# An fp32 encoder layer on two inputs: x passes ordered behind the short norm, head norms behind the next product, four early pairs, eight output tiles

## The chip, the cores and the metric

One core of one Trainium2 chip runs the whole program. The time is the device time of one execution in microseconds, median of several runs. "Profiled execution" is one more execution with the hardware profiler on; all durations below are from it. PE is TensorE, DVE VectorE, ACT ScalarE, POOL GpSimd, SP the engine that issues the DMAs.

## The reference, cut to what matters

Two inputs go through one transformer layer with the same weights: a long one (1024 tokens) and a short one (512), each with 16 meta tokens in front. All in fp32.

```python
def trunk(x, ...):
    h = concat([meta, x])                       # 16 + n tokens, 1024 wide
    n = rms_norm(h, g_mix);  proj = n @ w_in    # qa | ka | va | qb | kb | vb
    # A: 8 query heads, 2 key heads; q and k normed per head, rotated (axial)
    qa, ka = rope(rms_norm(qa)), rope(rms_norm(ka))
    oa = softmax(qa @ ka.T / 8) @ va
    # B: 4 heads, two softmax maps each, difference weighted by lambda; q and k rotated, no head norm
    ob = rms_norm((softmax(q1 @ k1.T / 8) - lam * softmax(q2 @ k2.T / 8)) @ vb) * (1 - lam_init)
    h = h + concat([oa, ob]) @ w_out
    n = rms_norm(h, g_ffn)
    gate = conv3(n @ w_ff_gate) + conv_b        # depthwise, along the tokens
    h = h + (gelu(gate) * (n @ w_ff_up)) @ w_ff_down   # 2816 wide
    return rms_norm(h, g_final)[:, 16:]
```

## The kernel before

Everything lies transposed: features on the 128 partitions, tokens along the free axis, 8 blocks of features (`KT`) for the width of 1024. An fp32 product is made of three matmuls in a faster format: each operand is split into a high part (a cast on ACT, `split`, L105) and a low part (the rest, a subtraction on DVE or POOL, L106), and `mm3` (L111 to L113) issues high x high, low x high, high x low. One product of a 128-wide column of a weight with a chunk of tokens is `dense`: 8 blocks, 24 matmuls into one PSUM tile.

`projection(s)` makes the 18 columns of w_in for input s (s = 1 is the short one, s = 0 the long one). It first reads x block by block: ACT writes `xhi` (L216) and the square of x (L220), DVE `xlo` (L217). For the short input the squares are summed by PE (L223), for the long one POOL adds them into `acc` (L225). `rsqrt_newton` (three ACT steps L95 to L97, two DVE steps L98 and L99) turns the sums into `rstd`, which DVE scales at L236. Only then can a product leave PSUM: DVE writes t = product * rstd (L277 for queries and keys of group A, L295 for values). For group A ACT squares t (L279), a matmul with `ones_hd` sums over the head (L281), `rsqrt_newton` runs again, and `rotary` (DVE, POOL) rotates; the results go to DRAM. The products of the short input take PSUM tiles of the tag s (3 tiles, sums in t, 2 tiles), those of the long one of the tag mm (2 tiles). A weight's column comes through one tile `w_f`, and `w_hi`, `w_lo` have two.

The program order is: projection of the short input; its attention merged with the long input's projection; the long input's attention merged with the short one's output product and gated network; the rest; and at the end `conv_glu_long`, the long input's gated network. A scheduler turns this into one fixed list per engine, by program order and its own model of durations; PSUM and SBUF tiles with their counts (`bufs`) limit how far apart things can move. `tc.issue_after(ins)` adds an edge: what is issued inside comes behind `ins` in its engine's list or waits for it. So the long input's passes may stand among the short norm's steps.

`conv_glu_long` works on pairs of 128 hidden features. For each pair it makes gate and up, and stores the product `act` and its sums (`a_t`, POOL) to DRAM. Then come seven products with blocks of w_down and of act over 11 pairs each (q = 0 to 6, a Strassen scheme; the last one in two halves of 256 tokens). For q = 0 the first two pairs' operands (left half of w_down, first half of act) are loaded ahead of the rest, into tiles `w_f` of the weight pool (L979, L980); those of the other pairs come as `a` and `a_f` (L995) behind the stores of the last pair. For q = 5 the second block of each pair from the third on is split into tiles that stay, and q = 6 uses these; the first two pairs are split again in q = 6, for each half. Last, `norm` writes y = h * gain * rs (L1066 and L1067 on ACT and POOL for every fourth, L1069 on DVE) into 4 tiles, each stored by its own DMA (L1070).

Of the kernel before, what the change touches and what calls it, by code (L numbers as in the profile page):

```python
# [12 lines left out]
F32 = mybir.dt.float32  # L13
# [76 lines left out]
def rsqrt_newton(g, tp, out, src, w, eps=None):  # L90
# [6 lines left out]
    nc.scalar.activation(out, y, AF.Square)  # L97
    nc.vector.scalar_tensor_tensor(out=out, in0=src, scalar=eps, in1=out, op0=ALU.add, op1=ALU.mult)  # L98
    nc.vector.scalar_tensor_tensor(out=out, in0=out, scalar=-3.0, in1=y, op0=ALU.add, op1=ALU.mult)  # L99

# [8 lines left out]
def mm3(g, ps, whi, wlo, xhi, xlo, start, stop):  # L109
    nc = g.nc  # L110
    nc.tensor.matmul(ps, lhsT=whi, rhs=xhi, start=start, stop=False)  # L111
    nc.tensor.matmul(ps, lhsT=whi, rhs=xlo, start=False, stop=False)  # L112
    nc.tensor.matmul(ps, lhsT=wlo, rhs=xhi, start=False, stop=stop)  # L113


def dense(g, ps, w, xhi, xlo, c0, cw, order=range(KT)):

    for i, k in enumerate(order):
        mm3(g, ps, *block(w, k), xhi[k][:, c0:c0 + cw], xlo[k][:, c0:c0 + cw], i == 0, i == KT - 1)
# [64 lines left out]
def projection(ctx, g, s, side, tag, tag2):  # L184
# [22 lines left out]
    with tc.tile_pool(name=f"ps{s}", bufs=2, side=side, reuse_waits="tile") as sp:  # L207
# [4 lines left out]
        for k in range(KT):  # L212
# [3 lines left out]
            nc.scalar.activation(xhi[k], x, AF.Copy, scale=gk)  # L216
            nc.vector.scalar_tensor_tensor(out=xlo[k], in0=x, scalar=gk,  # L217
                                           in1=xhi[k].bitcast(F32), op0=ALU.mult, op1=ALU.subtract)
            sq = acc if k == 0 and s == 0 else x
            nc.scalar.activation(sq, x, AF.Square)  # L220
# [8 lines left out]
        for i, (c0, cw) in enumerate(chunks):  # L229
# [5 lines left out]
            rsqrt_newton(g, sp, rstd[:, c0:c0 + cw], ps, cw)  # L235
        nc.vector.tensor_scalar(out=rstd, in0=rstd, scalar1=-0.5, scalar2=None, op0=ALU.mult)  # L236
# [24 lines left out]

    tab = load_tables(0)
# [4 lines left out]
    def qk_a(j):  # L267
        w = first if j == KA else load_weight(g, wp, g.w_in[j], ahead=1, lo_engine=nc.gpsimd if s == 0 else None)
        gn = g.gain[:, V_GK:V_GK + 1] if j == KA else g.gain[:, V_GQ:V_GQ + 1]
        for c0, cw in chunks:  # L270
            if j == KA and c0 == 0:
                ps = first_ps
            else:
                ps = g.psum.tile(P, cw, tag)
                dense(g, ps, w, xhi, xlo, c0, cw)
            t = tmp("t", cw, bufs=2 + s)
            nc.vector.tensor_tensor(out=t, in0=ps, in1=rstd[:, c0:c0 + cw], op=ALU.mult)  # L277
            sq = tmp("sq", cw, tag="w", bufs=2 + s)
            nc.scalar.activation(sq, t, AF.Square)  # L279
            ps = g.psum.tile(P, cw, tag2)  # L280
            nc.tensor.matmul(ps, lhsT=g.ones_hd, rhs=sq, start=True, stop=True)  # L281
            hn = tmp("hn", cw, bufs=1)
            rsqrt_newton(g, tp, hn, ps, cw)
            nc.vector.scalar_tensor_tensor(out=t, in0=t, scalar=gn, in1=hn, op0=ALU.mult, op1=ALU.mult)
            rotary(j, c0, cw, t, *tab)
            yield 25 * cw

    def values(j):
        w = load_weight(g, wp, g.w_in[j], ahead=1, lo_engine=nc.gpsimd if s == 0 else None)
        dst, tail = g.v[s][0 if j == VA else 1 + j - VB], g.vt[s][0 if j == VA else 1 + j - VB]  # L290
        for c0, cw in chunks:
            ps = g.psum.tile(P, cw, tag)
            dense(g, ps, w, xhi, xlo, c0, cw)
            t = tmp("t", cw, bufs=2 + s)
# [35 lines left out]
    for i in range(4):  # L330
        for j in (KB + i, QB + i):
            w = load_weight(g, wp, g.w_in[j], ahead=1, lo_engine=nc.gpsimd if s == 0 else None)
            for c0, cw in chunks:
                ps = g.psum.tile(P, cw, tag)
# [1016 lines left out]
```

## Time and profile before

| | |
|---|---|
| runs | 2161.72, 2146.39, 2156.50 us, median 2156.5 |
| profiled execution | 2160.32 us, span 2158.5 us |
| mean granted TensorE clock | 0.977 |
| busy share PE, DVE, ACT, POOL | 95%, 80%, 54%, 26% |
| DMA, mean over the span | 137 GB/s |

The profile shows one execution. "Busy" counts the time in which an engine works on at least one instruction; matmuls overlap, so the duration of one is longer than the distance to the next. A row of the timeline has the start, the duration, the engine, the line of the kernel, the operation, output <- inputs, shapes, how many rows it stands for, and in brackets how long the engine stood idle before it and who ended that. In the table of waits stand who waited <- for whom: us in total, times, the longest. In the table by stretches stand the stretch, its length, the busy time and the number of instructions of each engine, the granted TensorE clock (1.00 is full speed), DMA's share and rate.

### The profile page before, as it was taken

Reading aid. Unit: us, or ns where it says so; the run is one execution under the profiler, and the core shown is the slowest. Engines: PE = TensorE matmul, PEld = TensorE weight load, DVE = VectorE, ACT = ScalarE, POOL = GpSimd, SP = SyncE. Lnnn points to the kernel's source line nnn. Section 1 sums busy time; section 2 is a strip of 40 time slices with the busy share of each in tenths; the row PEclk is TensorE's granted clock in tenths of the full one; section 3 lists DMA queues with packets and bytes.
Section 4 is the critical chain, followed back from the end, with each engine's and each line's share of the span. In section 5 each row is a group of like instructions: output and inputs, shape, how many; then the busy total and the mean of one; then the engine's idle time right before and its main releaser. Section 6 shows DMA issues by size and latency. Waiting matters only on the chain.

```text
span 2158.5 us, 35229 instructions
## 1 busy us (share of the span) xinstructions
PE 2060.6 (95%) x12302; PEld 1840.5 (85%) x12302; DVE 1728.6 (80%) x3788; ACT 1161.2 (54%) x2255; POOL 552.3 (26%) x480
## 2 busy tenths in 40 slices
PE   7899998999999999999999999988999999989997
PEld 6898888898887999999989999887887777778877
DVE  6877888866979888889998885578778878869786
ACT  6534565543667565666666765345444344335454
POOL 3464222354112000000000000421444444420112
PEclk9999999899999999999999999998999999999999
DMA  6555334446631222223352234995222322257443
GB/s 233 169 173 186 112 115 141 147 168 220 207 118 54 95 74 75 73 77 119 103 186 85 83 112 139 273 289 192 98 98 83 108 103 83 104 185 243 118 127 123
DMA packets 171426, 296.31 MB, mean 137 GB/s; under 512 B 21456, under 2 KB 90608, under 8 KB 170736
## 3 DMA queue, kind: packets, MB, share of 16 engines
q1 hardware_dynamic: 171248, 294.05, 41.9%
q8 instruction: 97, 1.59, 0.3%
q14 instruction: 81, 0.66, 0.1%
HBM read 211.13 MB, written 82.85 MB: 136 GB/s over the span
## 4 chain that ended last, share of the span: by engine, by line
PE 73%; DVE 13%; DMA 6%; issue 3%; ACT 3%; POOL 1%; SPq 1%; POOLq 0%; DVEq 0%; ACTq 0%
PE ps_mm L111 17%; PE ps_mm L113 16%; PE ps_mm L112 16%; PE ps_t L411 5%; PE ps_s L386 3%; PE ps_s L387 3%; DVE w_lo L106 2%; PE ps_o L426 2%; PE ps_o L425 1%; DVE p L388 1%; PE ps_s L111 1%; PE ps_s L113 1%; PE ps_s L112 1%; DVE acc L921 1%; DVE pt_lo L106 1%
## 5 line engine op out<-in xcount | busy, mean ns | idle before, releaser
L111 PE MATMUL ps_mm<-xhi,w_hi 128*128 128x258 f32 (+3 forms) x1264 | 390.4, 309 | 11.8 <-ACT xhi L216 6.7
L112 PE MATMUL ps_mm<-xlo,w_hi 128*128 128x258 f32 (+3 forms) x1264 | 382.1, 302 | 3.0 <-DVE xlo L217 2.2
L113 PE MATMUL ps_mm<-xhi,w_lo 128*128 128x258 f32 (+3 forms) x1264 | 380.3, 301 | 0.3 <-DVE w_lo L106 0.3
L388 DVE TENSOR_SCALAR_CACHE_REDUCE p<-ps_s 114x344 f32<-114x344 f32 (+4 forms) x562 | 257.1, 489 | 42.1 <-PE ps_s L387 23.3
L111 PEld LDWEIGHTS ps_mm<-xhi,w_hi 128*128 128x128 f32 x1264 | 242.6, 192 | 18.5 <-ACT xhi L216 7.2
L105 ACT CAST pt_hi<-ps_t 128x512 fp32r<-128x512 f32 (+6 forms) x360 | 170.3, 484 | 162.7 <-PE ps_t L411 136.2
L393 ACT ACTIVATE p<-p,nm 114x1040 f32<-114x1040 f32 (+5 forms) x212 | 215.0, 1014 | 78.5 <-DVE nm L391 77.5
L106 DVE TENSOR_TENSOR w_lo<-w_f,w_hi 128x1024 fp32r<-128x1024 f32 (+1 forms) x176 | 187.1, 1069 | 77.8 <-ACT w_hi L105 77.4
L112 PEld LDWEIGHTS ps_mm<-xlo,w_hi 128*128 128x128 f32 x1264 | 242.5, 192 | 7.0 <-DVE xlo L217 2.6
L113 PEld LDWEIGHTS ps_mm<-xhi,w_lo 128*128 128x128 f32 x1264 | 241.9, 191 | 1.4 <-DVE w_lo L106 0.5
L105 ACT CAST w_hi<-w_f 128x1024 fp32r<-128x1024 f32 (+1 forms) x193 | 164.0, 863 | 94.4 <-PE ps_mm L112 54.1
L106 DVE TENSOR_TENSOR pt_lo<-ps_t,pt_hi 128x512 fp32r<-128x512 f32 (+4 forms) x312 | 172.0, 562 | 29.6 <-ACT pt_hi L105 28.7
L386 PE MATMUL ps_s<-k,q 128*114 128x348 f32 (+4 forms) x552 | 182.8, 336 | 12.1 <-DVE p L388 11.5
L106 POOL TENSOR_TENSOR a_lo<-gate,a_hi 128x256 fp32r<-128x256 f32 x44 | 43.5, 990 | 551.6 <-ACT a_hi L105 532.0
L411 PE MATMUL ps_t<-ident,p 128*128 128x128 f32 (+7 forms) x1188 | 182.5, 269 | 0.7 <-DVE pt_lo L106 0.2
L387 PE MATMUL ps_s<-k,q 128*114 128x348 f32 (+4 forms) x552 | 172.4, 317 | 0.1
L411 PEld LDWEIGHTS ps_t<-ident,p 128*128 128x128 f32 (+7 forms) x1188 | 140.3, 136 | 28.0 <-issue 6.6
L111 PE MATMUL ps_s<-xhi,w_hi 128*128 128x256 f32 (+4 forms) x480 | 148.5, 312 | 15.6 <-ACT xhi L216 7.3
L113 PE MATMUL ps_s<-xhi,w_lo 128*128 128x256 f32 (+4 forms) x480 | 146.8, 307 | 3.5 <-DMA w_lo<-wo 3.1
L112 PE MATMUL ps_s<-xlo,w_hi 128*128 128x256 f32 (+4 forms) x480 | 147.9, 309 | 0.3
L111 PE MATMUL ps_mm<-t_hi,w_hi 128*128 128x512 f32 (+2 forms) x368 | 143.5, 390 | 1.3 <-ACT t_hi L105 1.3
L112 PE MATMUL ps_mm<-t_lo,w_hi 128*128 128x512 f32 (+2 forms) x368 | 143.7, 390 | 0.5 <-DVE t_lo L106 0.5
(265 smaller groups left out, 5299.4 us busy)
## 6 DMA issues: line engine op xcount, KB each, us to landing
w_f<-w_gate SPq DMA_DIRECT2D x46, 512.0 KB, 3.3
w_f<-w_up SPq DMA_DIRECT2D x44, 512.0 KB, 3.4
w_f<-w_in SPq DMA_DIRECT2D x36, 512.0 KB, 3.9
a_f<-act SPq DMA_DIRECT2D x64, 256.0 KB, 2.9
w_f<-w_down SPq DMA_DIRECT2D x22, 512.0 KB, 3.3
act<-a_t SPq DMA_DIRECT2D x44, 256.0 KB, 2.1
a<-w_down SPq DMA_DIRECT2D x42, 256.0 KB, 5.4
w_hi<-wo SPq DMA_DIRECT2D x36, 256.0 KB, 5.2
```

Of the source, the lines that this page charges most:

```text
L105: nc.scalar.copy(hi, src)
L106: (lo_engine or nc.vector).tensor_tensor(out=lo, in0=src, in1=hi.bitcast(F32), op=ALU.subtract)
L111: nc.tensor.matmul(ps, lhsT=whi, rhs=xhi, start=start, stop=False)
L112: nc.tensor.matmul(ps, lhsT=whi, rhs=xlo, start=False, stop=False)
L113: nc.tensor.matmul(ps, lhsT=wlo, rhs=xhi, start=False, stop=stop)
L386: nc.tensor.matmul(ps, lhsT=q[0], rhs=k[:, c0:c0 + cw], start=True, stop=False)
L387: nc.tensor.matmul(ps, lhsT=q[1], rhs=k[:, c0:c0 + cw], start=False, stop=True)
L388: nc.vector.tensor_scalar(out=p[:, c0:c0 + cw], in0=ps, scalar1=HD ** -0.5, scalar2=-3.0e38, op0=ALU.mult, op1=ALU.max, accum_out=mx[:, i: ...
L393: nc.scalar.activation(p, p, AF.Exp, bias=nm, accum_out=l)
L411: nc.tensor.transpose(tps[:, c:c + M], p[:, k0:k0 + kw], g.ident[:M, :M])
L425: nc.tensor.matmul(o, lhsT=v[:, i, :], rhs=hi, start=i == 0, stop=False)
L426: nc.tensor.matmul(o, lhsT=v[:, i, :], rhs=lo, start=False, stop=False)
```

## The change

1. `mm3`, `dense` and `rsqrt_newton` return their last instruction. The short input's projection leaves the last ACT step of its norm and the scaling by DVE in `g.norm_of_short`, and the long input's xhi, xlo and squares are issued after these.
2. A new `product` issues a pending head norm behind the last matmul of the next product; so the norm of a chunk (L281 to rotary) is written one product later. t has 3 tiles for both inputs, the square has 2 of its own.
3. Four pairs' operands for q = 0 are loaded early instead of two, the third and fourth into a new pool. In q = 5 every pair's second block is split into tiles that stay (the first four into the tiles of the early operands), so that q = 6 splits no weight.
4. The final norm has 8 y tiles instead of 4.

```diff
 def rsqrt_newton(g, tp, out, src, w, eps=None):
...
-    nc.scalar.activation(out, y, AF.Square)
+    last = nc.scalar.activation(out, y, AF.Square).ins
...
+    return last
...
+            with ExitStack() as order:
+                for ins in g.norm_of_short:
+                    order.enter_context(tc.issue_after(ins))
+                nc.scalar.activation(xhi[k], x, AF.Copy, scale=gk)
+                nc.vector.scalar_tensor_tensor(out=xlo[k], in0=x, scalar=gk,
+                                               in1=xhi[k].bitcast(F32), op0=ALU.mult, op1=ALU.subtract)
+                sq = acc if k == 0 and s == 0 else x
+                nc.scalar.activation(sq, x, AF.Square)
...
+            last = rsqrt_newton(g, sp, rstd[:, c0:c0 + cw], ps, cw)
+        scaled = nc.vector.tensor_scalar(out=rstd, in0=rstd, scalar1=-0.5, scalar2=None, op0=ALU.mult)
+        g.norm_of_short = [last, scaled.ins]
...
+    pending = []
+
+    def product(w, c0, cw):
+        ps = g.psum.tile(P, cw, tag)
+        last = dense(g, ps, w, xhi, xlo, c0, cw)
+        if pending:
+            with tc.issue_after(last):
+                pending.pop()()
+        return ps
...
-                ps = g.psum.tile(P, cw, tag)
-                dense(g, ps, w, xhi, xlo, c0, cw)
-            t = tmp("t", cw, bufs=2 + s)
+                ps = product(w, c0, cw)
+            t = tmp("t", cw, bufs=3)
...
-            sq = tmp("sq", cw, tag="w", bufs=2 + s)
+            sq = tmp("sq", cw, bufs=2)
...
+            def norm(c0=c0, cw=cw, t=t, sq=sq):
+                ps = g.psum.tile(P, cw, tag2)
+                nc.tensor.matmul(ps, lhsT=g.ones_hd, rhs=sq, start=True, stop=True)
+                hn = tmp("hn", cw, bufs=1)
+                rsqrt_newton(g, tp, hn, ps, cw)
+                nc.vector.scalar_tensor_tensor(out=t, in0=t, scalar=gn, in1=hn, op0=ALU.mult, op1=ALU.mult)
+                rotary(j, c0, cw, t, *tab)
+
+            pending.append(norm)
...
+    for f in range(NPRE):
+        if f % 2 == 0:
+            first_w += halves(f, F32)
+            first_x += halves(f + 1, F32)
+        nc.sync.dma_start(out=first_w[f], in_=g.w_down[2 * f][:, :H])
+        nc.sync.dma_start(out=first_x[f], in_=g.act[f, 0])
...
-            y = op.tile([P, H], F32, name="y", tag="y", bufs=4)[:, :cw]
+            y = op.tile([P, H], F32, name="y", tag="y", bufs=8)[:, :cw]
...
-            w = last[f] if q == 6 and f > 1 else split_half(g, wp, w)
+            w = last[f] if q == 6 else split_half(g, wp, w)
...
+NPRE = 4
```

How it moves the lists. ACT at the start of the program, behind the short input's squares; 256 and 272 are the short norm's two chunks, 1040 the long input's passes, 1024 weight casts. Before:

```order
L216 ACTIVATE xhi_1914<-x,vec 128x1040
L220 ACTIVATE acc<-x 128x1040
L95 ACTIVATE rs_y<-ps_t,eps 128x256
L216 ACTIVATE xhi_1915<-x,vec 128x1040
L96 ACTIVATE rs_y<-rs_y 128x256
L97 ACTIVATE rstd<-rs_y 128x256
L220 ACTIVATE x<-x 128x1040
L95 ACTIVATE rs_y<-ps_t,eps 128x272
L105 CAST w_hi<-w_f 128x1024
L96 ACTIVATE rs_y<-rs_y 128x272
L105 CAST w_hi<-w_f 128x1024
L97 ACTIVATE rstd<-rs_y 128x272
```

And after:

```order
L95 ACTIVATE rs_y<-ps_t,eps 128x256
L96 ACTIVATE rs_y<-rs_y 128x256
L97 ACTIVATE rstd<-rs_y 128x256
L95 ACTIVATE rs_y<-ps_t,eps 128x272
L96 ACTIVATE rs_y<-rs_y 128x272
L97 ACTIVATE rstd<-rs_y 128x272
L223 ACTIVATE xhi_1914<-x,vec 128x1040
L227 ACTIVATE acc<-x 128x1040
L223 ACTIVATE xhi_1915<-x,vec 128x1040
L106 CAST w_hi<-w_f 128x1024 x2
```

The six steps of the norm now stand together, ahead of every long pass. DVE at the same place, first before:

```order
L217 SCALAR_TENSOR_TENSOR xlo_1922<-x,vec,xhi_1914 128x1040
L217 SCALAR_TENSOR_TENSOR xlo_1923<-x,vec,xhi_1915 128x1040
L98 SCALAR_TENSOR_TENSOR rstd<-ps_t,eps,rstd 128x256
L99 SCALAR_TENSOR_TENSOR rstd<-rstd,rs_y 128x256
L106 TENSOR_TENSOR w_lo<-w_f,w_hi 128x1024
L98 SCALAR_TENSOR_TENSOR rstd<-ps_t,eps,rstd 128x272
L99 SCALAR_TENSOR_TENSOR rstd<-rstd,rs_y 128x272
L217 SCALAR_TENSOR_TENSOR xlo_1924<-x,vec,xhi_1916 128x1040
L236 TENSOR_SCALAR rstd<-rstd 128x528
L277 TENSOR_TENSOR t<-ps_s,rstd 128x256
```

and after:

```order
L98 SCALAR_TENSOR_TENSOR rstd<-ps_t,eps,rstd 128x256
L99 SCALAR_TENSOR_TENSOR rstd<-rstd,rs_y 128x256
L98 SCALAR_TENSOR_TENSOR rstd<-ps_t,eps,rstd 128x272
L99 SCALAR_TENSOR_TENSOR rstd<-rstd,rs_y 128x272
L243 TENSOR_SCALAR rstd<-rstd 128x528
L224 SCALAR_TENSOR_TENSOR xlo_1922<-x,vec,xhi_1914 128x1040
L295 TENSOR_TENSOR t<-ps_s,rstd 128x256
L295 TENSOR_TENSOR t<-ps_s,rstd 128x272
```

One xlo stands between the scaling and the first t, where two xlo and a weight's rest stood ahead of the second chunk's steps. On PE, the nine matmuls of the long product (ps_mm) that stood ahead of the short input's next product are four.

PE at the long input's last key chunk (272 tokens); `ones_hd` is the head norm's matmul. Before:

```order
L111 MATMUL ps_mm<-xhi_1921,w_hi 128x272
L112 MATMUL ps_mm<-xlo_1929,w_hi 128x272
L113 MATMUL ps_mm<-xhi_1921,w_lo 128x272
L281 MATMUL ps_mm<-sq,ones_hd 128x272
L111 MATMUL ps_mm<-xhi_1914,w_hi 128x384
```

and after:

```order
L113 MATMUL ps_mm<-xhi_1921,w_hi 128x272
L114 MATMUL ps_mm<-xlo_1929,w_hi 128x272
L115 MATMUL ps_mm<-xhi_1921,w_lo 128x272
L407 MATMUL ps_s<-k,q 128x264 x3
L301 MATMUL ps_mm<-sq,ones_hd 128x272
```

The norm's matmul stood right behind its product; now score matmuls of the short input's attention stand between (three, in one row), and the first scores come some 75 rows earlier in PE's list, ahead of that much of the long input's projection.

SP at the seam from the last gate/up pair to the down products; the a_t and act rows are stores, a_0 to a_4 the other halves of w_down. Before:

```order
L962 DMA act_108<-act 128x512
L962 DMA act_108<-a_t 128x512
L995 DMA a_2_23039<-w_down 128x512
L962 DMA act_108<-a_t 128x512 x2
L995 DMA a_f<-act_108 128x512
L995 DMA a_3_23063<-w_down 128x512
```

and after:

```order
L982 DMA act_108<-a_t 128x512 x2
L1025 DMA a_4_23090<-w_down 128x512
L1025 DMA a_4_23092<-w_down 128x512
L982 DMA act_108<-a_t 128x512
L1025 DMA a_f<-act_108 128x512
L1025 DMA a_5_23116<-w_down 128x512
```

The first a_f behind the stores belonged to the third pair; now it belongs to the fifth, at the same place behind the last store.

51 lines of the change are left out of this document (22 added, 29 removed).

## The prediction

> **What bounds the kernel now.** I read the page first (shares of the engines), then the busy time by stretches, then what TensorE waits for in the first stretch, and last the instructions of the places that the diff touches.
>
> ```profile
> PE 2060.6 (95%) x12302; PEld 1840.5 (85%) x12302; DVE 1728.6 (80%) x3788; ACT 1161.2 (54%) x2255; POOL 552.3 (26%) x480
> ```
>
> TensorE (PE) is busy in 95% of the span, so a change that adds no matmul can win only what PE stands idle, 2158.5 - 2060.6 = 98 us, and what it runs at a lowered clock. I cut the head of the program at 183.25 us, where the first score matmul of an attention stands:
>
> ```profile
> core 0: us, PE busy (x) PEld busy (x) DVE busy (x) ACT busy (x) POOL busy (x), PEclk, DMA share, GB/s
> 7.31:183.25 175.94, 157.41 (x1103) 149.62 (x1104) 128.59 (x202) 89.13 (x165) 93.08 (x82) 0.96 0.58 190
> 183.25:510.00 326.75, 309.22 (x1950) 288.60 (x1951) 258.34 (x780) 175.89 (x426) 117.72 (x109) 0.95 0.43 140
> 510.00:900.00 390.00, 378.78 (x2522) 338.90 (x2521) 325.32 (x896) 236.77 (x412) 55.04 (x70) 0.99 0.36 115
> ```
>
> In the head PE idles 175.94 - 157.41 = 18.5 us, almost a fifth of all its idle time in a twelfth of the span. Who ends these waits:
>
> ```profile
> PE ps_mm L111 <- ACT xhi L216: 6.7, 2, 4.3
> PE ps_mm L281 <- ACT sq L279: 3.8, 1, 3.8
> PE ps_t L281 <- ACT sq L279: 2.5, 2, 1.8
> PE ps_mm L112 <- DVE xlo L217: 2.2, 1, 2.2
> PE ps_s L111 <- DVE t L295: 1.9, 1, 1.9
> ```
>
> (columns: us in total, times, longest). Two things that the diff moves stand here: the long input's passes xhi and xlo, and the head norm's matmul L281, which waits for the square of the product that has only just ended. Idle time is not all; the clock falls behind some of these waits:
>
> ```profile
> 30.20:40.40 10.20, 6.68 (x26) 5.98 (x27) 6.93 (x9) 4.89 (x6) 8.27 (x4) 0.50 0.51 156
> 129.20:132.60 3.40, 3.40 (x12) 3.28 (x11) 3.25 (x9) 1.77 (x4) 3.40 (x3) 0.50 0.21 66
> ```
>
> PE worked 6.68 and 3.40 us there at a clock of 0.50, which costs half of that, 3.3 and 1.7 us. So the head can give at most 18.5 + 5.0 = 23.5 us.
>
> **Part 1: the short norm ahead of the long passes.** Before, ACT runs long passes of more than 1 us each between the six steps of the short norm, and DVE does the same:
>
> ```profile
> 23.12 0.46 ACT L95 ACTIVATE rs_y<-ps_t,eps 128x256 f32<-128x256 f32 x1
> 23.48 1.15 ACT L216 ACTIVATE xhi<-x,vec 128x1040 fp32r<-128x1040 f32 x1
> 26.39 0.42 DVE L99 SCALAR_TENSOR_TENSOR rstd<-rstd,rs_y 128x256 f32<-128x256 f32 x1
> 26.97 0.47 ACT L95 ACTIVATE rs_y<-ps_t,eps 128x272 f32<-128x272 f32 x1
> 30.00 0.43 ACT L97 ACTIVATE rstd<-rs_y 128x272 f32<-128x272 f32 x1
> 30.17 2.67 POOL L106 TENSOR_TENSOR w_lo<-w_f,w_hi 128x1024 fp32r<-128x1024 f32 x1 [0.63 <-ACT w_hi L105]
> 30.55 0.49 DVE L98 SCALAR_TENSOR_TENSOR rstd<-ps_t,eps,rstd 128x272 f32<-128x272 f32 x1
> 31.07 2.06 DVE L99 SCALAR_TENSOR_TENSOR rstd<-rstd,rs_y 128x272 f32<-128x272 f32 x1
> 33.06 1.29 DVE L217 SCALAR_TENSOR_TENSOR xlo<-x,vec,xhi 128x1040 fp32r<-128x1040 f32 x1
> 34.27 0.42 DVE L236 TENSOR_SCALAR rstd<-rstd 128x528 f32<-128x528 f32 x1
> 34.73 0.77 DVE L277 TENSOR_TENSOR t<-ps_s,rstd 128x256 f32<-128x256 f32 x2
> 35.21 0.29 PEld L111 LDWEIGHTS ps_s<-xhi,w_hi 128*128 128x128 f32 x1 [0.30 <-DVE t L277]
> ```
>
> The last row is the start of the short value product, which takes a PSUM buffer that t has read. From the first step at 23.12, six steps of 0.43 to 0.47 end at about 25.8. DVE then has L98 of the second chunk (0.49), L99 (0.42 where POOL is quiet), the scaling (0.42), one xlo that the new order leaves there (1.29) and the first t (about 0.4): 25.8 + 3.0 = 28.8, and PE starts at about 28.9 where it started at 35.21. Of the long product only four matmuls stand ahead of it instead of nine. The five have to be done later: at about 0.17 us each, half of the 0.33 us of overlapping rows, that is 0.9 us. 35.21 - 28.9 - 0.9 = 5.4 us. Of the stretch at 0.50 the part behind 35.21 (5.2 us, so 2.6 us lost) may go too, if the shorter wait of 28.9 - 27.3 = 1.6 us no longer lowers the clock (PE's idle time began 4.27 us before 31.53). Rows of this trace stand on both sides:
>
> ```profile
> 58.94 0.44 PE L111 MATMUL ps_mm<-xhi,w_hi 128*128 128x384 f32 x1 [2.39 <-ACT xhi L216]
> 330.49 0.76 PE L435 MATMUL ps_o<-pt_hi,v_tail 64*128 64x512 f32 x1 [2.22 <-DVE pt_hi L106]
> 58.00:66.00 8.00, 7.06 (x54) 6.89 (x54) 7.22 (x9) 5.87 (x11) 4.61 (x4) 1.00 0.78 274
> 330.50:337.30 6.80, 6.80 (x22) 6.34 (x23) 4.14 (x16) 3.50 (x9) 0.88 (x2) 0.50 0.41 139
> ```
>
> After 2.39 us of waiting the clock stayed at 1.00, after 2.22 us it was 0.50 for 6.8 us. So I take half, 1.3 us, and the part gives **6.7 us** (bounds: 5.4 and 8.0). [...]
>
> The added waits: every long xhi and square now stands behind ACT's L97, every xlo behind DVE's scaling. Behind them on ACT are weight splits, which the order moves back by about one; nobody waits for the long sums (POOL's adds) before 69 us. I cost that at nothing; if PE does run out there, it is what the first rival prices.
>
> **Part 2: head norms behind the next product.** No instruction is added; L281 waits 3.8 + 2.5 = 6.3 us in the head for ACT's square. With a whole product (24 matmuls; the 12 of the stretch at 129.20 took 3.40 us at half clock, so 24 take some 3 us at the full one) ahead of it that square is done, since t and the square are short (0.77 us for two t above); the 2.5 us go. The 3.8 us stand at the long input's last chunk, and the stretch at 129.20 (1.7 us) follows them, 5.5 together; there the new order puts three score matmuls ahead of the norm's, not a product, so I count 4.5. **7.0 us**; below it 3, if the later norms only shift the long wait to the scores, above it 8. The other idle times of the head (2.39 for xhi, 1.9 for t) I leave as they are, since t has three buffers in the short input as before.
>
> **Part 3: four pairs early.** At the seam from the last gate/up pair to the down products:
>
> ```profile
> 1923.95 1.93 SPq L962 DMA_DIRECT2D act<-a_t  x2
> 1925.92 0.46 SPq L995 DMA_DIRECT2D a_f<-act  x1
> 1930.69 0.62 ACT L105 CAST w_hi<-a_f 128x512 fp32r<-128x512 f32 x1 [12.93 <-DMA a_f<-act]
> 1931.88 2.08 PE L111 MATMUL ps_mm<-w_hi 128*128 128x512 f32 x4 [6.29 <-ACT w_hi L105]
> 1932.85 0.62 ACT L105 CAST w_hi<-a_f 128x512 fp32r<-128x512 f32 x1 [1.02 <-DMA a_f<-act]
> 1928.00:1934.80 6.80, 2.92 (x7) 2.36 (x8) 2.59 (x4) 2.28 (x4) 0.00 (x0) 0.50 0.96 312
> ```
>
> PE has two pairs preloaded, ends them at 1931.88 - 6.29 = 1925.59, and waits for the third, whose load SP issues behind the stores of a_t. Two more pairs are 24 matmuls of 0.227 us (the spacing of the last pair's rows), 5.4 us, and PE ends at 1931.0. The first pair that is still loaded late keeps its place in SP's queue behind the same stores, so PE starts it at 1931.9 and waits 0.9 us. Then pairs come every 1932.85 - 1930.69 = 2.2 us, and PE needs 2.7. Gain 5.4 us; the half clock there cost 2.92 / 2 = 1.5 us, of which I count 0.6: **6.0 us** (5 to 6.9). The early loads add no bytes, they move 1 MB (four tiles of 256 KB) ahead of the last gate/up pairs, which hide it; if PE waited for all of it there, it would be 3.4 us at the 312 GB/s of the last row.
>
> **Part 4: eight output tiles, no second split.** The tail:
>
> ```profile
> 2147.34 0.47 ACT L95 ACTIVATE rs_y<-ps_mm,eps 128x256 f32<-128x256 f32 x1 [1.02 <-PE ps_mm L1140]
> 2149.78 1.74 DVE L1069 SCALAR_TENSOR_TENSOR y<-c,gain,rs 128x256 f32<-128x256 f32 x3
> 2154.41 0.51 ACT L1066 ACTIVATE y<-u,gain 128x256 f32<-128x256 f32 x1 [5.24 <-DMA yT<-y]
> 2154.99 0.72 POOL L1067 TENSOR_TENSOR y<-y,rs 128x256 f32<-128x256 f32 x1 [4.15 <-ACT y L1066]
> L1070 SPq DMA_DIRECT2D yT<-y x16: 332/332/1501, 2139.8 to 2155.7; - x16
> ```
>
> The last product ends before 2147 whatever the tiles do. With a tile each, DVE's six y (0.48 each) run from 2149.78 to 2152.7, and SP's eight issues of 0.33 to 0.45 end at 2153.3, where the last started at 2155.7: **2.7 us** (2 to 3.2). The dropped splits of the last product lie beside PE's matmuls on ACT and DVE: nothing.
>
> **Sum.** 6.7 + 7.0 + 6.0 + 2.7 = 22.4 us. From the profiled execution, 2160.3 us, that is 2137.9, a ratio of 0.9896; on the median of the runs, 2156.5 (3.8 lower), 2134. For 183 to 900 us, where the order is reshuffled too, no term: PE's idle time there is 17.5 + 11.2 us and the clock costs about 15 more, and nothing shows which way these go. I bound it at 10 us to either side, about a quarter.
>
> **Rivals.**
> (1) *The head's waits are replaced.* DVE is at 128.59 of 175.94 us, and POOL lengthens it: L99 took 0.42 us at 26.39, but 2.06 beside POOL's 2.67 us of w_lo, while L98, which reads PSUM, kept 0.49 beside the same instruction. Packing the head tighter puts more DVE steps beside POOL. If six that PE then waits for are longer by 1.64, 9.8 us come back: total 12.6, time 2144. Against it: DVE stays under 80% even in a head of 162 us. [...]
> (2) *The attentions gain too*, because norms queue behind products there as well: 10 us more, 2124.
> (3) *Slower: the softmax step p comes late.*
>
> ```profile
> PE ps_s L386 <- DVE p L388: 11.5, 8, 3.9
> ```
>
> (from 183 to 900 us) Norms and rotaries of the long input, now issued later, stand ahead of p on DVE. One such wait is 1.4 us, and with 6.8 us at 0.50 behind it 4.8. Ten more than the eight of now eat 22.4 and cost another 25: 2182. From five more on the gain is gone. Against it: DVE gets about 10 us of work more in 183 to 510 (0.73 of the 13.7 us), 82% instead of 79.
> (4) *It doesn't do what it says*: the new edges bind only the order of issue, and if what PE waits for in the head turns out to be the loads of the long input behind those passes, parts 1 and 2 give nothing and 3 and 4 give 8.7: 2148. Against it: the waits above name ACT and DVE, and DMA's share is 0.51 in 30.20 to 40.40.
>
> **How the numbers follow.** Forecast 0.54 (its own range 2126 to 2143), (1) 0.20, (2) 0.12, (3) 0.06, (4) 0.08. A measurement of this kernel tells about 1% from no change: faster means under 2135, slower over 2178. The forecast lies across the first of these, somewhat more than half below, so faster 0.54 x 0.55 + 0.12 + 0.05 of (1) = 0.47; same 0.46; slower 0.07. The range takes in (1), (2) and (4) with some room: 2118 to 2151.
>
> **What would show it.** Right: TensorE's idle time between 27 and 36 us falls from about 6.8 us to under 3; no wait of the head norm's matmul over 0.5; the 6.29 at the seam becomes about 1; no output step waits for a yT load; the first score matmul, with the long work done before it counted in, about 14 us earlier. Wrong: new waits on t, p or w_lo in 40 to 510 us, more stretches at 0.50 there, or a seam that waits for the split of pairs three and four.

## The result, and the profile after

| | before | changed |
|---|---|---|
| median of 11 runs | 2150.27 us (2146.39 to 2164.51) | 2142.05 us (2132.45 to 2146.66) |
| ratio | | **0.9941** (0.9918 to 0.9965) |
| profiled execution | 2160.32 us | 2142.05 us |

The change makes the kernel faster, by about 12.7 us (0.0059 of 2150), where 22.4 was forecast. The ratio is that of the means, 2140.7 and 2153.3 us; the medians alone differ by 8.2. The profiled execution from which the prediction counted lies 10 us over its kernel's median; so the 18.3 us between the two profiles overstate the change.

The page of the changed kernel, engines:

```profile
PE 2046.2 (96%) x12302; PEld 1830.6 (86%) x12302; DVE 1738.0 (81%) x3786; ACT 1158.9 (54%) x2253; POOL 556.1 (26%) x480
```

TensorE still sets the time. Its idle time went from 97.9 to 2140.2 - 2046.2 = 94.0 us only; its busy time fell by 14.4 us for the same 12302 matmuls. Part of that is granted clock: 99.5 us of its record lay at 0.50 before, 83.3 after. In the kernel before, rows of 272 columns follow each other at 0.227 us in the stretch at 0.50 from 35.6 us on and at 0.126 where the clock is 1.00; at that ratio 16.2 us less at half clock are worth 7.2 us, an estimate. Where the other 7 us of busy time went the two traces do not name.

By stretches, the changed kernel (the columns are those of the prediction's table):

```profile
27.00:36.00 9.00, 9.00 (x68) 8.79 (x69) 8.57 (x8) 7.36 (x12) 9.00 (x4) 1.00 0.49 155
40.00:50.00 10.00, 6.92 (x36) 6.87 (x37) 9.88 (x14) 5.82 (x9) 6.10 (x5) 0.66 0.60 211
183.00:480.00 297.00, 288.66 (x1875) 270.79 (x1874) 248.90 (x734) 167.52 (x404) 114.55 (x101) 0.98 0.45 144
480.00:550.00 70.00, 49.96 (x291) 44.62 (x289) 43.43 (x137) 31.18 (x66) 11.05 (x17) 0.80 0.63 211
```

and the kernel before in the last two:

```profile
183.00:480.00 297.00, 279.22 (x1745) 258.66 (x1746) 241.38 (x748) 165.62 (x402) 100.06 (x93) 0.95 0.45 143
480.00:550.00 70.00, 64.66 (x386) 60.25 (x384) 48.99 (x139) 30.38 (x62) 26.44 (x28) 0.93 0.68 234
```

Between 27 and 36 us TensorE no longer idles at all, the aim of part 1. But it idles 3.1 us of the ten from 40 on, and between 480 and 550, where the program passes from the short input's attention to the long one's, it stands idle for 20 us and runs at 0.80. The attention, for which the prediction had no term, went the other way: 130 more matmuls in the same 297 us.

Since the order on TensorE changed, I compare executions by work: each matmul weighs its width plus 8 columns (an estimate; at a clock of 1.00 rows of 256 columns follow each other at 0.118 us and rows of 512 at 0.227, 0.45 and 0.44 ns for each column so counted), and the **lead** of a kernel at a time is how much later the profiled execution of before had done the same amount (us). It is worked out from the records of each trace. The kernels with parts left out or mended, which the table lists too, are described under the experiments.

| profiled execution | 35 | 50 | 183 | 480 | 550 | 1900 | 1935 |
|---|---|---|---|---|---|---|---|
| changed | 8.9 | 2.8 | 1.2 | 22.6 | 7.0 | 11.7 | 15.8 |
| changed, again | 8.8 | 2.5 | 2.1 | 26.0 | 11.6 | 17.6 | 21.5 |
| changed without part 2 | 7.4 | 2.5 | -1.8 | 14.6 | 15.6 | 24.1 | 29.7 |
| the same, again | 8.7 | 3.9 | -3.4 | 13.8 | 13.9 | 18.1 | 24.0 |
| changed without part 1 | 0.2 | 1.4 | -5.9 | 0.2 | 1.8 | 5.2 | 11.3 |
| parts 3 and 4 alone | 0.2 | 0.4 | 0.3 | 7.2 | 7.3 | 15.7 | 21.7 |
| the same, again | 0.2 | 0.6 | -1.7 | -1.4 | -1.3 | 1.9 | 5.9 |
| sums of POOL left out | 9.0 | 12.1 | 1.7 | 8.5 | 7.0 | 21.3 | 24.9 |
| changed, seam mended | 8.7 | 3.7 | 4.6 | 27.8 | 16.3 | 18.5 | 24.2 |
| the same, again | 7.4 | 2.2 | -0.8 | 23.3 | 12.4 | 17.1 | 22.0 |

The two rows of parts 3 and 4 warn the reader: up to 1850 us those two executions and that of before have the same list on TensorE, and yet they lie up to 16 us apart. Differences below some 10 us count only where a pair of rows agrees.

The head, changed kernel. DVE, POOL and TensorE around the wait that eats the gain:

```profile
33.67 5.98 POOL L232 TENSOR_TENSOR acc<-acc,x 128x1040 f32<-128x1040 f32 x2
...
34.73 0.47 DVE L98 SCALAR_TENSOR_TENSOR hn<-ps_t,eps,hn 128x256 f32<-128x256 f32 x1
...
35.24 2.15 DVE L99 SCALAR_TENSOR_TENSOR hn<-hn,rs_y 128x256 f32<-128x256 f32 x1
...
37.31 3.43 DVE L107 TENSOR_TENSOR w_lo<-w_f,w_hi 128x1024 fp32r<-128x1024 f32 x1
...
42.49 0.44 DVE L316 TENSOR_TENSOR t<-ps_s,rstd 128x272 f32<-128x272 f32 x1
...
43.08 0.55 PE L113 MATMUL ps_s<-xhi,w_hi 128*128 128x256 f32 x1 [4.45 <-ACT xhi L223]
```

The next product takes the PSUM tile that t (L316) reads at 42.49. (The row names ACT's long xhi, which ended within a tenth of a microsecond of t, but which this product of the short input does not read.) That t stands on DVE behind L99 and w_lo, which took 2.15 and 3.43 us while POOL summed the long input's squares. L98, which reads PSUM, kept its 0.47. Part 2 has no share in this wait: it stands in the kernel without part 2 as well, 4.49 and 4.51 us in its two profiled executions. The second of these:

```profile
43.33 0.55 PE L113 MATMUL ps_s<-xhi,w_hi 128*128 128x256 f32 x1 [4.51 <-ACT xhi L223]
```

The wait of the short attention's scores for the softmax step p, first before, then changed, then without part 1, then without part 2, 183 to 480 us:

```profile
PE ps_s L386 <- DVE p L388: 10.1, 7, 3.9
```

```profile
PE ps_s L406 <- DVE p L408: 1.3, 4, 0.5
```

```profile
PE ps_s L405 <- DVE p L407: 9.3, 6, 3.0
```

```profile
PE ps_s L406 <- DVE p L408: 2.4, 5, 1.1
```

The seam between the attentions, changed kernel: SP's loads of w_out, then what ACT, DVE and TensorE do when the third arrives, and two stretches:

```profile
500.10 0.40 SPq L167 DMA_DIRECT2D w_f<-w_out  x1
501.09 0.38 SPq L167 DMA_DIRECT2D w_f<-w_out  x1
512.49 1.57 SPq L167 DMA_DIRECT2D w_f<-w_out  x2
```

```profile
521.68 1.04 ACT L106 CAST w_hi<-w_f 128x1024 fp32r<-128x1024 f32 x1 [11.24 <-DMA w_f<-w_out]
...
522.76 1.22 DVE L107 TENSOR_TENSOR w_lo<-w_f,w_hi 128x1024 fp32r<-128x1024 f32 x1 [10.72 <-ACT w_hi L106]
...
523.90 0.51 DVE L408 TENSOR_SCALAR_CACHE_REDUCE p<-ps_s 128x348 f32<-128x348 f32 x1
...
524.47 0.66 PE L406 MATMUL ps_s<-k,q 128*128 128x348 f32 x1 [11.73 <-DVE p L408]
```

```profile
502.50:529.80 27.30, 10.65 (x35) 9.24 (x36) 10.86 (x30) 9.04 (x16) 0.81 (x4) 0.50 0.98 346
512.50:521.70 9.20, 0.25 (x1) 0.00 (x0) 0.00 (x0) 0.02 (x1) 0.37 (x2) 0.50 1.05 397
```

The long attention's first scores were ready; the first p, which only has to read them, stood in DVE's list behind the split of the third w_out weight. That weight's load was issued at 512.49 among transfers that filled the DMA engines (share 1.05 at 397 GB/s) and its cast could start at 521.68. For 9.2 us TensorE worked 0.25 us and DVE not at all. This wait is new. It is not the cause of the whole stretch at half clock, which began at 502.5, ten us ahead of it.

The seam to the down products, and the tail, changed kernel:

```profile
1919.93 0.62 ACT L106 CAST w_hi<-a_f 128x512 fp32r<-128x512 f32 x1 [5.81 <-DMA a_f<-act]
...
1921.12 1.20 PE L113 MATMUL ps_mm<-w_hi 128*128 128x512 f32 x4 [1.99 <-ACT w_hi L106]
...
2130.35 0.47 ACT L95 ACTIVATE rs_y<-ps_mm,eps 128x256 f32<-128x256 f32 x1 [1.02 <-PE ps_mm L1175]
...
2132.79 2.21 DVE L1099 SCALAR_TENSOR_TENSOR y<-c,gain,rs 128x256 f32<-128x256 f32 x3
2132.99 1.73 POOL L1097 TENSOR_TENSOR y<-y,rs 128x256 f32<-128x256 f32 x2 [8.02 <-DVE rs L99]
```

The wait of 6.29 us became 1.99, and no output step waits for a store. From L95 to the end of the span it takes 2140.2 - 2130.35 = 9.9 us where it took 11.2.

### The profile page after: what moved, and what is told of

It is laid out like the page before. It is cut to its first block, busy times and chain, and to the rows that moved or that the text cites. A ratio compares the mean times of both kernels' runs of the same rounds, so it can differ in the third digit from the quotient of the medians.

```text
span 2140.2 us, 35200 instructions
## 1 busy us (share of the span) xinstructions
PE 2046.2 (96%) x12302; PEld 1830.6 (86%) x12302; DVE 1738.0 (81%) x3786; ACT 1158.9 (54%) x2253; POOL 556.1 (26%) x480
## 4 chain that ended last, share of the span: by engine, by line
PE 73%; DVE 14%; DMA 6%; issue 3%; ACT 3%; SPq 1%; POOL 0%; DVEq 0%; ACTq 0%; POOLq 0%
PE ps_mm L115 17%; PE ps_mm L113 17%; PE ps_mm L114 16%; PE ps_t L431 5%; PE ps_s L406 3%; PE ps_s L407 3%; DVE w_lo L107 2%; DVE p L408 2%; PE ps_o L446 1%; PE ps_o L445 1%; PE ps_s L113 1%; PE ps_s L115 1%; PE ps_s L114 1%; DVE acc L941 1%; DVE pt_lo L107 1%
## 5 line engine op out<-in xcount | busy, mean ns | idle before, releaser
L113 PE MATMUL ps_mm<-xhi,w_hi 128*128 128x258 f32 (+3 forms) x1264 | 383.2, 303 | 5.5 <-ACT xhi L106 1.6
L408 DVE TENSOR_SCALAR_CACHE_REDUCE p<-ps_s 114x344 f32<-114x344 f32 (+4 forms) x562 | 257.4, 489 | 32.9 <-PE ps_s L407 16.4
L107 DVE TENSOR_TENSOR w_lo<-w_f,w_hi 128x1024 fp32r<-128x1024 f32 (+1 forms) x182 | 195.8, 1082 | 78.5 <-ACT w_hi L106 76.2
L113 PEld LDWEIGHTS ps_mm<-xhi,w_hi 128*128 128x128 f32 x1264 | 240.2, 190 | 11.7 <-ACT xhi L106 3.9
L113 PE MATMUL ps_s<-xhi,w_hi 128*128 128x256 f32 (+4 forms) x480 | 149.3, 314 | 24.8 <-ACT xhi L223 11.7
```

What stands on the lines that cost most here:

```text
L107: (lo_engine or nc.vector).tensor_tensor(out=lo, in0=src, in1=hi.bitcast(F32), op=ALU.subtract)
L408: nc.vector.tensor_scalar(out=p[:, c0:c0 + cw], in0=ps, scalar1=HD ** -0.5, scalar2=-3.0e38, op0=ALU.mult, op1=ALU.max, accum_out=mx[:, i: ...
```

## The experiments

The theory after the result: part 1 gains; part 2 makes nothing shorter, since DVE limits the head, and costs at the seam. The rivals: POOL's sums are the whole trouble in the head; or the split at the seam is the whole trouble, and once it is put back all four parts pay. All edits are relative to the changed kernel, and each ratio is to the kernel before, run on the same chip.

**Without part 1**

```diff
-        g.norm_of_short = [last, scaled.ins]
```

> The changed kernel without its first part (the long input's passes may stand among the short norm's steps again); parts two, three and four stay. If part one is worth the 6.7 us of the prediction and nothing else hangs on it: 6 to 7 us slower than the changed kernel, lead over the kernel before at 35 us into the program 0 to 1 us instead of 8.9. If its gain is given back by DVE's steps beside POOL, as TensorE's wait of 4.5 us at 43 us suggests: 0 to 3 us slower, or not at all. If the seam of the attentions decides, the time depends on whether the wait of 11.7 us is there, and not on part one: without it 2125 to 2130.

Measured: 2147.5 us, ratio 0.9999 (0.9978 to 1.0019). That is 12 us behind the changed kernel (0.0058 of 2150), more than any of the three expectations allowed. Parts 2 to 4 together win nothing that can be told; the change's gain hangs on part 1.

**Without part 2**, every head norm is written at once again; part 2's tile counts of t and the square stay:

```diff
-            pending.append(norm)
+            norm()
```

> The changed kernel without its second part: each head norm is written right behind its own product, as before; parts one, three and four stay. If part two carried what the changed kernel wins in the short input's attention (some 20 us of lead between 183 and 400 us): that lead is gone, TensorE's waits for the head norm's square come back (6.3 us in the first 183 us), and the kernel is about 10 to 20 us slower than the changed one without the seam's wait, so about 2145 to 2160. If the lead there comes from the earlier start of the attention (part one): it stays at 15 us or more, 2135 to 2145.

Measured: 2128.09 us, 0.9914 (0.9887 to 0.9940), the fastest kernel of the study. Both expectations had it at 2135 or more. Taking the late norms away makes the kernel no slower, and by the median faster; the two intervals still overlap here, and the repetition below bears on it. Its lead is -1.8 us at 183 us, and it loses nothing at the seam.

**Six of the seven sums on POOL left out**, the sum of squares being incomplete then:

```diff
-            elif k:
+            elif k == KT - 1:
```

> The changed kernel without six of the seven adds of squares of the long input on POOL (its sum of squares is left incomplete). DVE's and ACT's lists are the changed kernel's up to about 42 us. If POOL's adds lengthen DVE's steps there (L99 2.15 us instead of 0.42, the weight's rest 3.43 instead of 1.23): these go back to 0.45 and 1.25, and TensorE's wait of 4.45 us at 43 us is under 1 us, the stretch at half clock there gone, the lead at 50 us 6 to 9 us instead of 2.8. If DVE is late there only because more work stands in its list: durations as before, wait over 3 us.

Measured: one execution, 2133.38 us. The same three DVE steps and TensorE's wait:

```profile
35.08 0.43 DVE L99 SCALAR_TENSOR_TENSOR hn<-hn,rs_y 128x256 f32<-128x256 f32 x1
...
35.63 1.23 DVE L107 TENSOR_TENSOR w_lo<-w_f,w_hi 128x1024 fp32r<-128x1024 f32 x1
...
38.63 0.44 DVE L316 TENSOR_TENSOR t<-ps_s,rstd 128x272 f32<-128x272 f32 x1
...
39.13 0.39 PE L113 MATMUL ps_s<-xhi,w_hi 128*128 128x256 f32 x1 [0.48 <-DVE t L316]
```

So POOL's additions do lengthen DVE's steps: 0.43 for 2.15, 1.23 for 3.43, and 4.45 us of waiting become 0.48. The lead at 50 us is 12.1 where it was 2.8. But at 183 us it is 1.7, as in the changed kernel: further on in the head TensorE waits for other things (2.43 us for the long norm's rstd at 147.62, with 10.2 us at half clock, 3.66 us for the load of q at 152.93). POOL's sums explain the wait at 43 us, not that the head as a whole gives nothing.

**Part 2 away and the sums late**, each behind the first rotary step on POOL:

```diff
-            pending.append(norm)
+            norm()
...
-                nc.gpsimd.tensor_tensor(out=acc, in0=acc, in1=x, op=ALU.add)
+                with tc.issue_after(g.first_u[0]):
+                    nc.gpsimd.tensor_tensor(out=acc, in0=acc, in1=x, op=ALU.add)
```

> Experiment 3's kernel (parts one, three and four) with POOL's adds of the long input's squares put behind POOL's first rotary step of the short input. Nothing is left out. If POOL beside DVE is what makes TensorE wait 4.5 us at 43 us: DVE's L99 there takes 0.45 us, the weight's rest 1.3, the wait is under 1.5 us, the lead at 50 us 6 to 9 us. The sums then stand where DVE has other work, so part of it may come back by 183 us; total 2122 to 2130 if it does not, 2128 to 2134 if it does. If the wait is due to the amount of DVE work: no change at 43 us.

Measured: 2136.87 us, 0.9931 (0.9907 to 0.9956): no faster than without part 2 alone. 2122 to 2134 had been expected. The wait at 39.49 is 0.81 us, and then, in this kernel:

```profile
60.51 0.69 PE L114 MATMUL ps_mm<-xlo,w_hi 128*128 128x384 f32 x1 [4.58 <-DVE xlo L224]
```

A wait of the old length came back 20 us later, for DVE's xlo, and the lead is 9.9 at 50 us and -4.7 at 183. The head's waits are moved by such an order, not removed.

**Parts 3 and 4 alone**: part 1 and part 2 as in the two edits above undone, with the tile counts of t and the square that the kernel before has.

> The kernel before with the third and fourth part alone (four early pairs, no second split, eight output tiles). By the prediction 8.7 us (6.0 at the seam to the down products, 2.7 in the tail). By the lead of the kernels with these parts over the kernel before, read behind and ahead of the two places, 5.4 to 6.1 at the seam and 1 to 1.9 in the tail, 6 to 8 us: ratio 0.9965 (0.994 to 0.999), 2140 to 2144. A rival: the early loads delay the last gate/up pairs, then the lead at 1900 us is below that at 1500 us by over 2 us. With experiments 1 to 3 it is the fourth corner: if part one and part two acted independently, this kernel should be as much slower than the one without part one as the one without part two is slower than the mended seam, that is between 2135 and 2150 whatever part two does.

Measured: 2144.51 us, 0.9975 (0.9952 to 0.9997).

**The seam mended.** The splits of the attention's output and of the third and later w_out weights come behind the long attention's twelfth p and fourth exponential; its first four softmax tiles are written ahead of what the merge puts there:

```diff
-            w = load_weight(g, wp, g.w_out[j], bufs=wb)
+            with ExitStack() as order:
+                if j > 1:
+                    order.enter_context(tc.issue_after(g.first_p[11]))
+                    order.enter_context(tc.issue_after(g.first_e[3]))
+                w = load_weight(g, wp, g.w_out[j], bufs=wb)
...
-        merge(attention(es0, g, 0, "right"), R2[0], f1, R2[1])
+        a0 = attention(es0, g, 0, "right")
+        for _ in range(4):
+            next(a0)
+        merge(a0, R2[0], f1, R2[1])
```

> The changed kernel with the order at the seam of the two attentions mended: the long attention's first four softmax tiles are written ahead of the short input's output product, and the splits of that product's operands (third weight on, and all of m) stand behind the twelfth softmax step p on DVE and the fourth exponential on ACT. Theory A (the missing gain was given back at the seam, where DVE's p stood behind the split of the third w_out, whose load landed 9 us late): TensorE's wait of 11.7 us and most of the 27 us at half clock go, some 15 to 20 us less than the changed kernel, 2122 to 2128, ratio to the kernel before 0.985 to 0.988. Theory B (at the seam TensorE waits for the loads of q, k and v themselves, DMA being full at 400 GB/s, and the split in front of p is incidental): the wait changes its name and stays within 3 us, time 2138 to 2145, ratio about 0.994.

Measured: 2135.06 us, 0.9942 (0.9922 to 0.9962), the ratio of the changed kernel; 0.985 to 0.988 was expected if the split were the whole trouble, about 0.994 if not. Its repetition below shows what is left at the seam.

**All mended**: all four parts, the seam mended (now for all of the w_out weights, not from the third on) and the sums late.

> All four parts, with the seam of the attentions mended (as experiment 1, now for all of the output product's weights) and POOL's sums later (as experiment 6). If part two is a gain that only the seam and POOL took back: below experiment 3, 2115 to 2125, with a lead over the kernel before of 25 us or more at 480 us that is kept to 600 us. If part two itself moves the long projection's end ahead of the short attention's end, and TensorE lacks work there whatever stands at the seam: lead at 480 us 25 us or more, at 550 us 8 to 12 us less, total 2126 to 2136, no better than experiment 3.

Measured: 2131.75 us, 0.9927 (0.9897 to 0.9956): between the changed kernel and the one without part 2, and not to be told from either. Its lead goes from 16 us at 480 us to 12 at 550; the 25 that both expectations had for 480 us are not there.

**Four kernels again, on one chip**, since the differences are small: the changed kernel, without part 2, seam mended, parts 3 and 4 alone.

> The changed kernel itself, on the same chip and beside the next three, since the differences in question (5 to 13 us) are as large as what two executions of one list of instructions differ by. If the parts act as the ratios so far say (part one -13 us, part two +5.5, three and four -5.4): 0.994, slower by 5 to 14 us than the kernel without part two and by 3 to 8 than the one with the mended seam. If those differences came from the chips and the luck of executions: all three within 3 us of each other.

> Experiment 3's kernel again (parts one, three and four), to be set against the changed kernel on one chip: 0.991, 2126 to 2132, if part two costs time; equal to the changed kernel within 3 us if not.

> Experiment 1's kernel again (all four parts, seam of the attentions mended), against the changed kernel on one chip: 5 to 9 us below it if the seam's wait of 11.7 us is there in most executions and the mending removes most of it; within 3 us of it if the wait is made up elsewhere.

> Experiment 5's kernel again (parts three and four alone): with part one alone on top of it being experiment 9's kernel, the difference of the two is part one's worth. 13 us by the ratios so far, 6.7 by the prediction. Against the kernel before: 5 us less (0.9975), 8.7 by the prediction.

| | median us | ratio | interval |
|---|---|---|---|
| changed | 2137.18 | 0.9943 | 0.9922 to 0.9965 |
| without part 2 | 2133.12 | 0.9918 | 0.9897 to 0.9939 |
| seam mended | 2135.39 | 0.9932 | 0.9912 to 0.9952 |
| parts 3 and 4 alone | 2141.99 | 0.9961 | 0.9940 to 0.9981 |

On this chip the kernel without part 2 is again the fastest, 4 to 5 us ahead of the changed one. The mended seam stays within 3 us of the changed kernel, as was expected if its wait is made up elsewhere, not the 5 to 9 of the other case.

The seam in the changed kernel again, in that without part 2, and in the mended one, first rows of waits, then 480 to 550 us:

```profile
519.96 0.66 PE L406 MATMUL ps_s<-k,q 128*128 128x348 f32 x1 [11.40 <-DVE p L408]
```

```profile
480.00:550.00 70.00, 62.56 (x372) 55.27 (x371) 51.79 (x160) 35.05 (x68) 19.05 (x23) 0.95 0.70 231
```

```profile
505.37 1.39 PE L522 MATMUL ps_o<-o_sq,ones_v 128*128 128x306 f32 x2 [2.64 <-ACT o_sq L520]
510.26 1.21 PE L406 MATMUL ps_s<-k,q 128*128 128x348 f32 x3 [2.27 <-DMA q<-qk]
522.29 0.49 PE L406 MATMUL ps_s<-k,q 128*128 128x348 f32 x1 [2.30 <-DVE p L408]
```

```profile
480.00:550.00 70.00, 57.78 (x321) 48.70 (x320) 50.23 (x155) 34.75 (x72) 11.12 (x16) 0.88 0.63 213
```

The wait for p is there in both profiled executions of the changed kernel (11.73 and 11.40); in those of the mended one it is 2.92 and 2.30. TensorE is busy 57.78 us in the mended one, against 49.96 with the wait and 62.56 without part 2. So mending the split brings back about 8 of the 12.6 us of busy time that the changed kernel is short of here. But busy time at half clock is less work (0.227 us for a row of 272 columns that takes 0.126 at the full one), and the lead gives the split less. By 508 us, before any wait for p, the lead has fallen by 8 to 10 us in all four executions, two of the changed kernel and two of the mended one, to between 14.6 and 17.6. From there to 550 us the changed kernel loses another 7.6 and 4.0 us, the mended one 1.3 and 2.3. The larger part of the loss is not the split but, as far as these rows tell, that little is left to fill with. The short attention's scores, first in the changed kernel, then without part 2 (first and last start in us):

```profile
L406 PE MATMUL ps_s<-k,q x144: 278/284/578, 164.4 to 446.9; 128*128 128x264 f32 x64, 128*102 128x264 f32 x48, 128*104 128x264 f32 x32
```

```profile
L406 PE MATMUL ps_s<-k,q x144: 278/285/569, 169.6 to 428.0; 128*128 128x264 f32 x64, 128*102 128x264 f32 x48, 128*104 128x264 f32 x32
```

Without part 2 the attention ends 19 us sooner, and more products of the long projection are left over for the seam: of its 1296 matmuls 156 and 162 start after 480 us, the last at 508 and 509, where the two profiled executions of the changed kernel have 99 and 79, the last at 498 and 494. With part 2 they were used up in the attention, where they show as a lead of 22.6 at 480 us, and they are missing 30 us later.

**Head norms late for the short input only**

```diff
-            pending.append(norm)
+            if s == 1:
+                pending.append(norm)
+            else:
+                norm()
```

> The changed kernel with the pending head norms in the short input's projection alone; the long input's norms are written at once, as before. In its lists the weights of the output product stand behind the long attention's first p again (with pending norms in the long input's projection alone they stand ahead of it). If part two's loss comes from the long input's norms alone: no wait over 3 us at the seam of the attentions, TensorE's waits for the head norm's square in the first 183 us shorter than with norms at once, and 0.991 or less (2122 to 2131), no worse than experiment 9. If the pending norms of the short input cost time in the head (later rotaries, later keys): 0.9925 to 0.995, and a lead over the kernel before at 183 us below that of experiment 9 (-3 us).

Measured: 2133.71 us, 0.9920 (0.9899 to 0.9940), as without part 2; and the lead goes from 10.5 at 480 us to 13.1 at 550, with no loss at the seam. So by this one profiled execution it is the long input's late norms that bring the loss there, and the short input's late norms bring nothing that can be seen.

## Why the prediction was right or wrong

The total fell inside the range, on the forecast side, at half the size. That was luck in part: part 1 gave some 4 us more than its term and part 2 some 12 less, and the two errors have opposite signs. The terms did not come out as the sum had them:

| | predicted us | shown, as whole time |
|---|---|---|
| parts 3 and 4 | -8.7 | -5.4 and -8.4 (0.9975, 0.9961) |
| part 1 added to these | -6.7 | -11 (0.9968 to 0.9916, means of two) |
| part 2 added last | -7.0 | **+5.6** (0.9916 to 0.9942) |

Part 2 measured without part 1 says the same: 0.9968 becomes 0.9999, 6.7 us. The tile counts of t and the square belong to part 2, but they came into the kernels with the second row's step, since the edit without part 2 kept them; so that row is part 1 and the tile counts together. The edit that takes part 1 alone out of the changed kernel has no such mixture and gives 12 us. By the intervals of the ratios the two values for part 2 are each known to 5 or 6 us either way: a gain of 3 us, the prediction's bound, is excluded by either, and a loss is what both point to.

- **Part 2, the step that failed.** The waits for the square, of which the sum counted 2.5 whole and 4.5 of 5.5 with its stretch at half clock, went as foreseen: no wait of the head norm's matmul is left in the head of the changed kernel. But I counted a wait that goes as time won, on an engine list whose next instruction needed DVE as well. Other waits stand there (2.71 for t at 172.81, 2.23 for a weight at 123.10, and part 1's 4.45 at 43 us); TensorE's idle time up to the point of 182 us is 16.4 us after 18.5. Between 8 and 183 us it is 16 us with the late norms and 19 without, so they win some 3 us there, and their lead at 183 us is 1 to 2 us where the kernel without them has -2 to -3: too little to be sure of, and far from 7.0. The bound "3, if the later norms only shift the long wait" stopped above zero without a reason. And the sum had **no term for 183 to 900 us**, where the changed kernel gave back some 15 us of lead at one seam, and the kernel without part 2 none.
- **Part 1** did at its place what was worked out, and more: the short value product started at 27.61 us instead of 35.21 (28.9 predicted), and the lead at 35 us is 8.9. As a gain of the head it was wrong: at 183 us the kernels with part 1 have leads from -5 to 4.6, none that can be told from nothing. That it is worth 11 us all the same comes from the attention. With part 1 the scores wait 1.3 to 4.1 us for p between 183 and 480, and leads grow by 16 to 24 us there, in every kernel with POOL's sums in full, with part 2 or without it. Without part 1 they wait 7.9 to 10.1, and leads grow by 7 at most. Half clock there falls from 30.7 us to 10.2 or less, but one execution without part 1 (parts 3 and 4 alone, the first) has 10.2 as well. The first score came at 164.4 us instead of 183.3, 18.9 earlier (but 5.0 by work done, where I had said 14). An earlier start alone does not explain it: with POOL's sums left out the scores begin at 152.9 and still wait 7.9 us for p, and without part 1 they begin at 162.9 and wait 9.3. So the gain needs part 1 in the kernels tried, but the short waits for p can be missing with part 1 in place. How part 1 gets p in time was not tried by itself.
- **Part 3** was right in mechanism: 6.29 became 1.99 where I had 0.9. The casts of the fifth pair's two operands ended at 1920.55 and 1921.07 and TensorE started at 1921.12, so against the end of the preloaded pairs these loads came about 1 us later than I had. The half clock went by half in this execution (3.4 us at 0.50 from 1922.5, where it was 6.8), and between 1900 and 1935 the lead grows by 3.6 to 6.1 us in every row of the table, for a forecast of 6.0.
- **Part 4** gave 1.3 us from L95 to the end, not 2.7: DVE's first three y took 2.21 us together, 0.74 each instead of the 0.48 that I took, beside POOL's 1.73 us of y. The same lengthening that I had weighed for the head I left out here.
- **The rivals.** (1) was right for the head, in kind and place: DVE's steps beside POOL, by 1.7 and 2.2 us. (2) was right on the attention, with twice its size, but mostly not by its reason: kernels without late norms gain 16 to 19 us there too. (3) named p late on DVE; it came at one place, 11.7 us with 27.3 us at half clock around it, and what stood ahead of it was the split of a weight, not the norms and rotaries. All three came true together, and their sum happens to lie near (1)'s 2144, which is luck.
- **Clock.** The length of a wait alone does not decide here whether the clock is halved behind it: in the changed kernel the wait of 1.99 us at 1921.12 has 3.4 us at 0.50 behind it, while one of 2.06 us at 1435.24, for a load of w_lo, has 1.00 before and behind it. All recorded stretches at 0.50 ahead of the tail, 15 in the profiled execution of before and 14 in that of the changed kernel, last 3.4, 6.8, 10.2 or 27.3 us. What starts one was not shown.

What stays open: how part 1 gains in the attention, and whether part 2's tile counts have a share in it; where part 2 costs its 6.7 us when part 1 is absent, since that kernel has no such seam (lead 0.2 at 480 us, 1.8 at 550); and whether a seam with both the split mended and filler kept would make all four parts the best. The seam mended alone was not told apart from the changed kernel.

The fastest version is the changed kernel without part 2: 0.9914 and 0.9918, measured twice. Its medians of 2128 and 2133 us lie below before's (2150) and, less surely, below the changed kernel's (2142, and 2137 on the same chip).

## What to carry to other kernels

In this kernel, removing a wait of the busiest engine won only what the next instruction on that engine could use; before counting it, look for the engine that feeds that next one, and for an engine whose work beside it makes its steps longer (here L99 took 2.15 us beside POOL's sums and 0.43 without them). Work that fills gaps is a stock: an order that uses it earlier shows a gain there and a hole where it was before, so follow the lead to the next seam and beyond. And on a fixed list, a step that depends on a late load should not stand ahead of the step on which the bottleneck depends.

## What the runs showed of the hardware

- **DVE behind POOL.** In the changed kernel three DVE steps of two SBUF inputs ended 1.1 us after the POOL instruction beside them: w_lo began at 37.31, POOL's two additions ended at 33.67 + 5.98 = 39.65, and w_lo ended at 40.74, 1.1 us later, about what it takes without them (1.23); w_lo from 29.11 and xlo from 31.85 ended at 31.46 and 34.80, where POOL ended at 30.38 and 33.72. This looks as if DVE had stood still until POOL was done; the rows show no more than the starts and ends. For these three steps the price follows what was left of POOL's instruction (2.2 us for the w_lo from 37.31, 3.43 less 1.23), not a factor on DVE's. It is not so beside every POOL instruction: in the kernel before, DVE's w_lo from 50.01 took 1.22 us beside an addition on POOL that began at 50.05, and it was the addition that took longer, 3.52 us for the 2.39 of the one at 27.16.
- **One list, many times.** Two profiled executions with the same instructions (parts 3 and 4 alone) took 2136.5 and 2152.9 us, with 55.5 and 101.0 us of the clock's record at 0.50 (mean granted clock 0.987 and 0.977); the changed kernel's took 2136.4 and 2142.1 with 60.0 and 83.3 (0.986 and 0.981). From 183 to 480 us the first pair had 0.98 and 0.95, with seven waits for p in each, 7.9 and 10.1 us in total.
- **A load** of 512 KB that takes 3.5 us as a median in the changed kernel (w_in) took 9.2 us at the seam until its cast could start, with the DMA engines at a share of 1.05 and 397 GB/s.
